# First part of a hybrid-encoder step on one core: TensorE and VectorE taken from the list scheduler and given the order of the source, rewritten as explicit pipelines

## The chip, the core and the metric

The kernel runs on one core of a Trainium2 chip. The metric is the device time of one execution in microseconds (us); the median of 3 runs of the kernel before is 1809.56 us (1807.75 to 1811.77). Below, PE is TensorE, DVE is VectorE, ACT is ScalarE, POOL is GpSimd and SP is SyncE, which issues most of the DMAs.

## The reference

One layer of an encoder is applied to 1024 prompt rows and to 32 rows of a running stream, 1056 rows of 1024 features. All is float32.

```
xn   = rmsnorm(h)
u_a, u_b, v_b, q, k, v, gates = split(xn @ w_in)       # 256,256,256,512,512,512,3*1024
y_a  = GLU(gelu(S5(u_a)))          # 16 groups x 64 complex states, zero-order hold, + d*u
y_b  = u_b * (tril(W_s) @ layernorm(v_b) + b_s)        # chunks of 128 positions, 4 groups
z    = q @ k.T / 8                                     # 8 heads x 64, strictly causal
y_c  = (exp(log_sigmoid(z) + sum of log_sigmoid(-z) over the keys in between)) @ v
h    = h + (sum_i sigmoid(gates_i) * (y_i @ W_i)) @ w_out
h    = h + (silu(rmsnorm(h) @ w_gate) * (.. @ w_up)) @ w_down;   out = rmsnorm(h)
```

The new states, keys, values and normalised v_b rows are outputs too.

## The kernel before, in words

**Numbers.** Every float32 operand of a dense product is split into a rounded high part and the rest (wh and wl for weights, split by ACT at L120 and POOL at L121 out of the buffer raw; xnh and xnl for the normalised rows). A product takes three matmuls (L147, L148, L149). A weight unit is read by SP (L116 or L119), split, and kept in a ring of 4 buffers. "Feature-major" products have up to 512 rows as moving columns (chunks of 512, 272 and 272 rows, 24 matmuls each); "token-major" ones have 256 weight columns (blocks of 128 rows, 24 matmuls each).

**The first part** (the context ph1, up to about 700 us) has these stages:

- norm: per block of 128 rows, DVE scales (L184), PE transposes (L189), ACT copies the high half, DVE subtracts (L194). Then the values: 8 blocks and the sample rows, token-major; ACT writes them to a DRAM buffer v_d.
- keys and queries: four tasks (qk0 to qk3), feature-major; DVE subtracts (qe, L335), SP writes k_d and q_d; keys are transposed back (L310) for the output (kt, L312).
- S5 set-up: some 300 small DVE operations, all issued through the line L455 (the function pump), which end in the tile big; PE transposes big (L629) and craw (L638); later matmuls build KK (L666, L667), and 16 DMAs spread it to D (L684).
- sgu: nine token-major blocks of v_b; DVE normalises each into VN (L412). Beside them runs a chain over the 8 heads: SP loads a head's values and the same values shifted by one row (vda, vdt, L377 and L378), DVE subtracts neighbours (L385, L387), ACT rounds (L388), DVE subtracts (L389), SP writes the head to dv_d (L390). vda and vdt have one buffer each. Then, twice, PE computes u_b (UB) and the mixing pm (L434, L437), for which the PSUM pool "z" has 2 buffers, and DVE forms yt from it (L441, L445).
- ua and s5_main: u_a (ua, L698), the S5 scan and its GLU (yl, za).
- attention: 32 units (pairs of heads x 4 pairs of row blocks x 2), each with scores (PE, ACT sigmoid, DVE scan L862), transposes (L884), the split of the weights (DVE L893) and the product with the head's differences (L901, L902); one sample step near the end (L967 to L1020).

**What fills the gaps.** fill(us) puts steps of the waiting tasks (the keys and queries, then 33 gate products kept for later in DRAM) into the instruction stream; pump puts set-up operations of DVE there.

**What sets the order.** A list scheduler with priorities orders the instructions of all engines after they are written down; it may take a ready instruction ahead of one written earlier. The second part (from L1083 on) is the same in both kernels.

Of the kernel before, what the change touches and what calls it, by code (L numbers as in the profile page):

```python
# [48 lines left out]
def trunk_kernel(ctx: ExitStack, tc: tile.TileContext,  # L49
# [132 lines left out]
    def norm_T(wk, psp, tag, src, dst, gb, rows, hl, off, pair=None):  # L182
        r = rms_rstd(wk, src, rows)
        v.scalar_tensor_tensor(dst, src, r, gb[0:rows], op0=OP.mult, op1=OP.mult)  # L184
        for q in range(2):
            pt = psp.tile([128, 512], F32, name="ptn", tag=tag, bufs=2)
            for e in range(4):
                k = 4 * q + e
                pe.transpose(pt[:, 128 * e:128 * e + rows], dst[:, 128 * k:128 * k + 128], ident[0:rows, 0:rows])  # L189
            pv = pt.rearrange("p (a b) -> p a b", b=128)[:, :, 0:rows]  # L190
            hi = hl[0][:, 4 * q:4 * q + 4, off:off + rows]
            s.activation(hi, pv, AF.Copy)
            lo = hl[1][:, 4 * q:4 * q + 4, off:off + rows]
            v.tensor_sub(lo, pv, hi.bitcast(F32))  # L194
            if pair is not None:
                g.tensor_copy(pair[:, 4 * q:4 * q + 4, 0:32], hi.bitcast(F32))
                g.tensor_copy(pair[:, 4 * q:4 * q + 4, 32:64], lo.bitcast(F32))

    def half_tile(p, name, tag, dt=F32R):
# [7 lines left out]
    with ExitStack() as ph1:  # L207
        ps1 = ph1.enter_context(pool("ps1", 2, PSUM))
        rings.append(ph1.enter_context(pool("ring1", 4)))
        qk = ph1.enter_context(pool("qk", 1))  # L210
        kk = ph1.enter_context(pool("kk", 1))
# [23 lines left out]
        v_units = []  # L235
        with pool("p0", 1) as p0:
            gmix = p0.tile([128, 1024], F32, name="gmix")
            for b in (0, 1, 2, 3, 4, 5, 8, 6, 7):
                t0, rows, h, off = BLOCKS[b]
                xt = p0.tile([128, 1024], F32, name="xt", bufs=3)  # L240
                sp.dma_start(xt[0:rows], x_rows(b))
                if b == 0:
                    sp.dma_start(gmix, dram_bcast(norm_mix, 1024))
                if b < 2:
                    v_units.append(tm_units(win, 1792 + 256 * b))
                xg = p0.tile([128, 1024], F32, name="xg", bufs=2)
                norm_T(p0, ps1, "t", xt[0:rows], xg[0:rows], gmix, rows, xn[h], off, xn2 if b == 8 else None)


        def v_dense(wk):  # L250
            us = v_units
            share = -(-len(pending) // 45)
            z = wk.tile([1, 128], F32, name="vz")
            v.memset(z, 0.0)
            for i in range(4):
                sp.dma_start(v_d[i][0:1, :], z)
            for b, hc in [(b, hc) for b in range(6) for hc in range(2)] + [(b, hc) for hc in range(2) for b in (8, 6, 7)]:
                t0, rows, h, off = BLOCKS[b]
                pump(share)
                if b == 8:  # L260
                    ps = ps_dense()[0:64, 0:256]
                    tm_sample(ps, xn2, us[hc])
                    vs = wk.tile([32, 256], F32, name="v32", bufs=2)
                    add_pair(vs, ps, vs)
                    sp.dma_start(sb_v_s[0, 0, 4 * hc:4 * hc + 4].rearrange("h t d -> t h d"),
                                 vs.rearrange("t (h d) -> t h d", d=64))
                    sp.dma_start(vs_d[:, 256 * hc:256 * hc + 256], vs)
                    continue
                ps = ps_dense()[0:rows, 0:256]
                tm_dense(ps, xn[h], off, rows, us[hc])  # L270
                tc.cur_priority -= SOONER
                v32 = wk.tile([128, 256], F32, name="v32", bufs=2)
                s.activation(v32, ps, AF.Copy)
                s.dma_start(sb_v_p[0, 0, 4 * hc:4 * hc + 4, t0:t0 + 128].rearrange("h t d -> t h d"),
                             v32.rearrange("t (h d) -> t h d", d=64))
                for i in range(2):
                    s.dma_start(v_d[2 * hc + i][1 + t0:129 + t0, :], v32[:, 128 * i:128 * i + 128])
                tc.cur_priority += SOONER
# [17 lines left out]
        def qk_dense(wk, hp):  # L296
# [64 lines left out]
        def sgu(wk, WT, BB, gs):  # L361
# [31 lines left out]
            us = tm_units(win, 512)  # L393
            for b, (t0, rows, h, off) in enumerate(BLOCKS):
# [23 lines left out]
                if b < 8:  # L418
                    load_values(b)
            for ft in range(2):  # L420
                UB = wk.tile([128, T], F32, name="UB", bufs=1)
                unit = fm_unit(win, 256 + 128 * ft)
                for h, o, n, t0 in CHUNKS:
                    ps = ps_dense()[:, 0:n]
                    fm_dense(ps, unit, xn[h], o, n)
                    s.activation(UB[:, t0:t0 + n], ps, AF.Copy)
                for q in range(3):
# [19 lines left out]
                    sp.dma_start(y_d[2 + ft][min(q, 1)][:, o:o + w], yt[:, 0:w])  # L447

# [18 lines left out]
        def s5_setup(pl, keep, out):  # L467
# [7 lines left out]
            v.tensor_copy(rows[32:40, :].rearrange("a (g2 p) -> a g2 p", p=64), lt[32:40, :, None].to_broadcast([8, 2, 64]))  # L475
# [130 lines left out]
            braw = pl.tile([128, 2, 8, 16], F32, name="braw")  # L606
            for n, b in enumerate((ssm_b_re, ssm_b_im)):
                sp.dma_start(braw[:, n], bass.AP(tensor=b.tensor, offset=b.offset, ap=[[16, 128], [2048, 8], [1, 16]]))
# [22 lines left out]
            craw = pl.tile([128, 2, 128], F32, name="craw")  # L631
            for n, c in enumerate((ssm_c_re, ssm_c_im)):
                for g2 in range(2):
                    sp.dma_start(craw[:, n, 64 * g2:64 * g2 + 64],
                                 bass.AP(tensor=c.tensor, offset=c.offset + g2 * 1024, ap=[[2048, 8], [64, 16], [1, 64]]))
# [34 lines left out]
            dr = pl.tile([8, 32], F32, name="dr")  # L670
            sp.dma_start(dr, ssm_d[0].rearrange("(gp c) -> gp c", c=32))
# [15 lines left out]
        def ua_dense(wk):  # L687
            for ft in range(2):
                unit = fm_unit(win, 128 * ft)
# [11 lines left out]
                sp.dma_start(us_d[128 * ft:128 * ft + 128], ua)  # L701

        def s5_main(pl, S):
# [72 lines left out]
            fill(24)  # L776
# [34 lines left out]
        def attention(at, qk_tasks):  # L811
# [28 lines left out]
            def stage_a(hp, tp, h2):  # L840
                kst = heads[hp, h2][0]
                q2 = qs.pop((hp, tp, h2))
                ws = []
                for tt in range(2):
                    i = 2 * tp + tt
                    n = 128 * (i + 1)
                    cs = ((0, max(n, 256)),) if n <= 512 else (((0, 384), (384, 256)) if n == 640 else
                                                             ((0, 384), (384, 384)) if n == 768 else
                                                             ((0, 512), (512, n - 512)))
                    om = at.tile([128, 1024], F32, name="om", bufs=4)  # L850
                    for c0, w in cs:
                        z = ps_tile("z")
                        last = c0 + w >= n
                        pe.matmul(z[:, 0:w], q2[:, 0, 128 * tt:128 * tt + 128], kst[:, c0:c0 + w], start=True, stop=False)
                        pe.matmul(z[:, 0:w], q2[:, 1, 128 * tt:128 * tt + 128], kst[:, c0:c0 + w], start=False, stop=not last)
                        if last:
                            d0 = n - 128 - c0
                            pe.matmul(z[:, d0:d0 + 128], identb, maskb, start=False, stop=True)
                        e = min(w, n - c0)
                        s.activation(om[:, c0:c0 + e], z[:, 0:e], AF.Sigmoid, scale=-0.125)  # L860
                    rev = om[:, 0:n][:, ::-1]
                    v.tensor_tensor_scan(rev, rev, rev, 1.0, op0=OP.mult, op1=OP.bypass)  # L862
                    ws.append(om)
                    yield ws, 2 * n / 2400.0 + 0.06
# [3 lines left out]
            def stage_b(hp, tp, h2, ws):  # L868
                vt = heads[hp, h2][1]
                if h2 == 0:  # L870
# [3 lines left out]
                hl = {}  # L874

                def turn(p):

                    pt = ps_tile("t")
                    diag = p == tp
                    for e in range(4):  # L880
                        if diag and e == 0:
                            continue
                        sb, tt = 2 * p + 1 - e // 2, e % 2
                        pe.transpose(pt[:, 128 * e:128 * e + 128], ws[tt][:, 128 * sb:128 * sb + 128], ident)  # L884
                    lo = 128 if diag else 0
                    if diag:
                        wh, wl = diags[cnt[0] % 2]
                        cnt[0] += 1
                    else:
# [434 lines left out]
```

## Time and profile before

| what | us |
|---|---|
| median of 3 runs | 1809.56 (1807.75 to 1811.77) |
| profiled execution, its own time | 1813.32 |
| its span, first to last instruction | 1811.5 |
| PE busy | 1695.1 (94%) |
| DVE, ACT, POOL busy | 697.2, 516.6, 553.9 |

PE is busy 94% of the span, so a stage is read by the time that PE does not work in it and by what ends that wait. The last stage of the first part ends near 700 us; from there on the two kernels have the same program. "Granted clock" is the share of TensorE's full clock that the chip allowed in a stretch.

### The profile page before, as it was taken

The page shows a single profiled execution, that of the slowest core. Times are in us where ns is not written, and L with a number is a line of the kernel's source. Part 1 is how long each engine was busy: PE and PEld are TensorE (multiplying, and loading weights), DVE is VectorE, ACT ScalarE, POOL GpSimd, SP SyncE. Part 2 cuts the span into 40 slices and gives each one's busy share as a digit, 9 for nine tenths or more (in the row PEclk, how much of TensorE's full clock was granted, in tenths as well). Part 3 has the DMA queues.
Part 4 walks back from the last instruction along what each step waited for, and adds up shares of the span by engine and source line. Part 5 has one row for each costly group of instructions (what it writes and reads, how often), then busy time and mean ns, then how long its engine had stood idle before and what let it go on. Part 6 is the DMA issues. An engine that isn't in the chain of part 4 may idle for free.

```text
span 1811.5 us, 25687 instructions
## 1 busy us (share of the span) xinstructions
PE 1695.1 (94%) x10421; PEld 1503.5 (83%) x10421; DVE 697.2 (38%) x1371; ACT 516.6 (29%) x906; POOL 553.9 (31%) x349
## 2 busy tenths in 40 slices
PE   6989959899899997988999899999999999999997
PEld 6978858677679995788999899889889889888885
DVE  7953621532675651730256601230230220321315
ACT  5322322233555542212323322112112112111124
POOL 2210201243112205435443233233323333333334
PEclk9999979999999998988999999999999999999999
DMA  7454766254655424633362211111111111111102
GB/s 219 119 131 111 186 187 144 94 153 146 192 158 154 124 84 121 222 116 108 105 203 68 73 48 47 47 37 51 41 36 48 46 47 47 47 47 47 47 25 96
DMA packets 242736, 182.12 MB, mean 101 GB/s; under 512 B 59380, under 2 KB 220184, under 8 KB 242616
## 3 DMA queue, kind: packets, MB, share of 16 engines
q1 hardware_dynamic: 214056, 165.25, 31.3%
q10 hardware_dynamic: 28560, 15.21, 2.8%
q8 instruction: 82, 1.34, 0.3%
q14 instruction: 38, 0.31, 0.1%
HBM read 138.66 MB, written 41.18 MB: 99 GB/s over the span
## 4 chain that ended last, share of the span: by engine, by line
PE 49%; DVE 3%; DMA 3%; issue 3%; POOL 2%; ACT 1%; POOLq 0%; SPq 0%; ACTq 0%
PE p L149 16%; PE p L148 16%; PE p L147 16%; POOL wl L121 1%; DMA raw<-y_d 1%; PE p L1266 1%; DVE rs_m L172 1%; DMA raw<-in_w_out_dram 1%; POOL y L1137 1%; DVE rs_m L173 1%; DMA raw<-in_w_branch_c_dram 0%; DMA raw<-in_w_in_dram 0%; PE ptn L189 0%; DVE xb L184 0%; ACT wh L120 0%
## 5 line engine op out<-in xcount | busy, mean ns | idle before, releaser
L121 POOL TENSOR_TENSOR wl<-raw,wh 128x1024 fp32r<-128x1024 f32 x164 | 400.3, 2447 | 871.2 <-ACT wh L120 799.8
L148 PE MATMUL p<-x,wh 128*128 128x272 f32 (+1 forms) x1056 | 342.3, 324 | 0.0
L147 PE MATMUL p<-x,wh 128*128 128x272 f32 (+1 forms) x1056 | 341.5, 323 | 0.0
L149 PE MATMUL p<-x,wl 128*128 128x272 f32 (+1 forms) x1056 | 341.4, 323 | 0.0
L120 ACT ACTIVATE wh<-raw 128x1024 fp32r<-128x1024 f32 x164 | 172.2, 1058 | 445.9 <-PE p L149 182.5
L1222 DVE TENSOR_TENSOR sl<-p,sl 128x272 f32<-128x272 f32 (+1 forms) x66 | 34.6, 525 | 463.8 <-PE p L149 463.8
L147 PEld LDWEIGHTS p<-x,wh 128*128 128x128 f32 x1056 | 198.8, 188 | 16.0
L148 PEld LDWEIGHTS p<-x,wh 128*128 128x128 f32 x1056 | 198.8, 188 | 15.9
L149 PEld LDWEIGHTS p<-x,wl 128*128 128x128 f32 x1056 | 198.5, 188 | 15.3
L147 PE MATMUL p_d<-xnh,wh 128*128 128x272 f32 (+1 forms) x464 | 165.0, 356 | 22.1 <-ACT ua L698 16.0
L149 PE MATMUL p_d<-xnh,wl 128*128 128x272 f32 (+1 forms) x464 | 157.6, 340 | 7.7 <-POOL wl L121 7.7
L148 PE MATMUL p_d<-xnl,wh 128*128 128x272 f32 (+1 forms) x464 | 156.5, 337 | 0.0
L1225 POOL TENSOR_TENSOR act<-sl,act 128x512 fp32r<-128x512 f32 (+2 forms) x66 | 61.0, 924 | 279.6 <-ACT act L1223 279.6
L1276 DVE TENSOR_TENSOR h<-p,h 128x512 f32<-128x512 f32 x160 | 108.2, 687 | 79.3 <-PE p L149 79.3
L148 PE MATMUL p<-wl,act 128*128 128x512 f32 x352 | 137.2, 390 | 1.2 <-POOL wl L121 1.2
L149 PE MATMUL p<-wh,act 128*128 128x512 f32 x352 | 137.1, 389 | 0.0
L147 PE MATMUL p<-wh,act 128*128 128x512 f32 x352 | 136.9, 389 | 0.0
L147 PEld LDWEIGHTS p_d<-xnh,wh 128*128 128x128 f32 x464 | 91.9, 198 | 31.0 <-ACT ua L698 16.4
L862 DVE TENSOR_TENSOR_SCAN om<-om 128x128 f32<-128x128 f32 (+3 forms) x64 | 93.5, 1470 | 30.6 <-ACT om L860 30.4
L149 PEld LDWEIGHTS p_d<-xnh,wl 128*128 128x128 f32 x464 | 91.4, 197 | 16.4 <-POOL wl L121 9.4
L148 PEld LDWEIGHTS p_d<-xnl,wh 128*128 128x128 f32 x464 | 91.6, 197 | 6.7
L1223 ACT ACTIVATE act<-sl 128x272 fp32r<-128x272 f32 (+1 forms) x66 | 32.5, 492 | 191.1 <-DVE sl L1222 191.1
(351 smaller groups left out, 3351.6 us busy)
## 6 DMA issues: line engine op xcount, KB each, us to landing
raw<-in_w_in_dram SPq DMA_DIRECT2D x66, 512.0 KB, 4.0
raw<-in_w_gate_up_dram SPq DMA_DIRECT2D x44, 512.0 KB, 3.8
raw<-in_w_down_dram SPq DMA_DIRECT2D x22, 512.0 KB, 3.5
q<-q_d SPq DMA_DIRECT2D x64, 128.0 KB, 3.1
raw<-in_w_out_dram SPq DMA_DIRECT2D x16, 512.0 KB, 4.5
dv_d<-vdt SPq DMA_DIRECT2D x8, 768.0 KB, 4.3
vt<-dv_d SPq DMA_DIRECT2D x8, 768.0 KB, 6.6
sig_d<-sga ACTq DMA_DIRECT2D x21, 256.0 KB, 2.5
```

Source lines behind the costliest of these rows:

```text
L120: s.activation(wh, raw, AF.Copy)
L121: g.tensor_sub(wl, raw, wh.bitcast(F32))
L147: pe.matmul(ps, ah, bh, start=start, stop=False)
L148: pe.matmul(ps, ah, bl, start=False, stop=False)
L149: pe.matmul(ps, al, bh, start=False, stop=stop)
L172: v.scalar_tensor_tensor(t, y, mh, y, op0=OP.mult, op1=OP.mult)
L173: v.scalar_tensor_tensor(y, t, 1.5, y, op0=OP.add, op1=OP.mult)
L862: v.tensor_tensor_scan(rev, rev, rev, 1.0, op0=OP.mult, op1=OP.bypass)
L1222: v.tensor_mul(sl[:, 0:n], pu, sl[:, 0:n])
L1223: s.activation(act[:, e, t0:t0 + n], sl[:, 0:n], AF.Copy)
L1225: g.tensor_sub(act[:, e, T + TS + t0:T + TS + t0 + p], sl[:, 0:p], act[:, e, t0:t0 + p].bitcast(F32))
L1276: v.tensor_add(hr[:, cs], ps, hr[:, cs])
```

## The change

The first part runs under a manual schedule for PE and DVE: these two engines execute in the order in which the source issues the work. ACT, POOL and SP are still ordered by the list scheduler. The source is rewritten so that this order is a pipeline: the norm of block i+1 is issued ahead of the transposes of block i and the values of block i-1; the S5 set-up's DVE operations start after the norm and stand beside the key and query tasks; the attention issues, per step, a transpose group, the next unit's scores, the held product and a constant amount of gate work. The ring of weight units gets 5 buffers instead of 4, some weights are requested one unit earlier, the small set-up DMAs are issued at its start, and the sample step stands behind the last attention unit.

```diff
     with ExitStack() as ph1:
+        ph1.enter_context(tc.manual_schedule(engines={mybir.EngineType.PE, mybir.EngineType.DVE}))
-        rings.append(ph1.enter_context(pool("ring1", 4)))
+        rings.append(ph1.enter_context(pool("ring1", 5)))
...
+            for i, b in enumerate(order):          # first_norm; takes in v_dense as values(b)
+                if i + 1 < len(order):
+                    scale(order[i + 1])
+                if i + 3 < len(order):
+                    load(order[i + 3])
+                norm_turn(ps1, "t", xgs.pop(b)[0:rows], rows, xn[h], off, xn2 if b == 8 else None)
+                if i:
+                    values(order[i - 1])
...
             def load_values(i):
-                va = wk.tile([128, 12, 64], F32, name="vda")
-                vt = wk.tile([128, 12, 2, 64], F32R, name="vdt")
+                va = vk.tile([128, 12, 64], F32, name="vda")
+                vt = vk.tile([128, 12, 2, 64], F32R, name="vdt")
...
             VN = wk.tile([128, 9, 256], F32, name="VN")
-            us = tm_units(win, 512)
...
+                if b == 7:
+                    unit = fm_unit(win, 256)
...
-            fill(24)                               # s5_main
+            fill(28)
...
-                        fill(1.3)
+                        fill(0.6)
...
+            beside = 2.0                           # attention
+            ws = [scores(units[0], 0), scores(units[0], 1)]
+            fill(2)
+            held = None
             for i, u in enumerate(units):
                 ahead(i + 2)
+                nxt = units[i + 1] if i + 1 < len(units) else None
+                wn = []
+                part = beside / (u[1] + 2)
+                for p in range(u[1] + 1):
+                    now = turn(u, ws, p)
+                    if nxt and len(wn) < 2:
+                        wn.append(scores(nxt, len(wn)))
+                    if held:
+                        apply(*held)
+                    held = now
+                    fill(part)
+                if nxt and len(wn) < 2:
+                    wn.append(scores(nxt, len(wn)))
+                fill(part)
+            fill(2)
+            apply(*held)
+            sample_attention(at, ck)
...
             while tasks and credit[0] > 0:
-                pump(5)
+                pump(3)
...
+                fill(7)
                 next(setup)
                 finish(qk_tasks[1])
+                next(setup)
+                finish(qk_tasks[2])
                 for _ in setup:
                     pass
+                us = tm_units(win, 512)
+                finish(qk_tasks[3])
```

What stands where is best seen in three places of the engines' queues (a row is a line of the source, the operation, output<-inputs and the tile's shape). The first is DVE's queue around the first complex products of the S5 set-up, Pr and Pi. Before, they stand among the last rows of the norm:

```order
L184 SCALAR_TENSOR_TENSOR xg<-xt,rs_m,gmix 128x1024
L194 TENSOR_TENSOR xnl_150<-ptn,xnh_149 128x4x128 x2
L455 TENSOR_TENSOR sm<-sm 128x8 x2
L455 TENSOR_TENSOR Pr<-sm 128x8
L455 TENSOR_TENSOR Pi<-sm 128x8
L455 TENSOR_TENSOR sm<-sm 128x8
L455 TENSOR_TENSOR te<-Pr 128x8
L455 TENSOR_TENSOR te<-Pi 128x8
```

Now the same products stand among the subtractions of the keys and queries (qe, L357), and the set-up's line is L481:

```order
L481 TENSOR_TENSOR Pr<-sm 128x8
L481 TENSOR_TENSOR Pi<-sm 128x8
L481 TENSOR_TENSOR te<-Pr 128x8
L481 TENSOR_TENSOR te<-Pi 128x8
L481 TENSOR_TENSOR Pr<-te 128x8
L481 TENSOR_TENSOR te<-Pr,Pi 128x8
L357 TENSOR_TENSOR qe<-p_av,qe 128x272
```

The set-up's work has moved behind the norm, and its operations stand in the order of the source, each behind the one that it needs.

The second is PE's queue where it transposes big and craw. Before, eight of the sixteen transposes of big stand after the first matmuls of qk1, and matmuls of qk1 between them and the rest:

```order
L147 MATMUL p_av<-xnh_147,wh 128x512
L148 MATMUL p_av<-xnl_148,wh 128x512
L149 MATMUL p_av<-xnh_147,wl 128x512
L629 MATMUL p_z<-ident,big 128x128 x8
L147 MATMUL p_av<-xnh_147,wh 128x512
L629 MATMUL p_z<-ident,big 128x128 x8
L148 MATMUL p_av<-xnl_148,wh 128x512
L638 MATMUL p_z<-ident,craw 128x128 x2
```

Now all of qk0 and qk1 and three matmuls of qk2 stand ahead of them, and the sixteen are in one piece (L663):

```order
L147 MATMUL p_av<-xnh_147,wh 128x512
L148 MATMUL p_av<-xnl_148,wh 128x512
L149 MATMUL p_av<-xnh_147,wl 128x512
L663 MATMUL p_z<-ident,big 128x128 x16
L667 MATMUL p_z<-ident,craw 128x128 x2
L147 MATMUL p_av<-xnh_147,wh 128x512
L148 MATMUL p_av<-xnl_148,wh 128x512
```

About one key and query task more lies ahead of these transposes.

The third is DVE's queue at the first two yt of the sgu stage (numbers behind a name are its buffer's; each head has its own vda). Before, the third head's differences stand ahead of the first yt, and the fourth head's behind the second:

```order
L412 SCALAR_TENSOR_TENSOR VN_1892<-vb_2442,rs_m_2468,gs_488 32x256
L385 TENSOR_TENSOR vda_2077<-vda_2077,vdt_2078 128x512
L387 SCALAR_TENSOR_TENSOR vda_2077<-vdt_2078,last_1890,vda_2077 128x256
L389 TENSOR_TENSOR vdt_2078<-vda_2077,vdt_2078 128x12x64
L441 TENSOR_TENSOR yt_2592<-p_z_2583,BB_487 128x512
L445 TENSOR_TENSOR yt_2592<-yt_2592,UB_2498 128x512
L441 TENSOR_TENSOR yt_2605<-p_z_2596,BB_487 128x512
L445 TENSOR_TENSOR yt_2605<-yt_2605,UB_2498 128x512
L385 TENSOR_TENSOR vda_2153<-vda_2153,vdt_2154 128x512
```

Now the differences ahead of the first yt are the eighth and last head's:

```order
L433 SCALAR_TENSOR_TENSOR VN_2369<-vb_2878,rs_m_2904,gs_1017 32x256
L407 TENSOR_TENSOR vda_2865<-vda_2865,vdt_2866 128x512
L409 SCALAR_TENSOR_TENSOR vda_2865<-vdt_2866,last_2367,vda_2865 128x256
L411 TENSOR_TENSOR vdt_2866<-vda_2865,vdt_2866 128x12x64
L466 TENSOR_TENSOR yt_3024<-p_z_3015,BB_1016 128x512
L470 TENSOR_TENSOR yt_3024<-yt_3024,UB_2930 128x512
L466 TENSOR_TENSOR yt_3037<-p_z_3028,BB_1016 128x512
```

Every yt stands behind all eight heads.

Lines of the new kernel that are named below, with those of the kernel before in brackets: L399 and L400 (L377, L378) loads of a head, L407 to L411 (L385 to L389) its differences, L466 and L470 (L441, L445) yt, L481 (L455) set-up, L663 (L629) transposes of big, L889 (L862) scans, L912 (L893) the split of the attention weights.

## Rows read from the trace of the kernel before

**Rows 1.** Windows: stretch, its length, busy us (instructions) per engine, granted clock, DMA share, GB/s.

```profile
26.00:79.00 53.00, 51.61 (x426) 50.05 (x425) 50.81 (x273) 20.47 (x43) 7.89 (x7) 1.00 0.56 147
79.00:160.00 81.00, 72.82 (x468) 65.72 (x467) 40.45 (x80) 22.20 (x44) 15.61 (x8) 0.96 0.48 121
160.00:304.00 144.00, 119.22 (x771) 108.20 (x770) 58.17 (x163) 40.31 (x94) 21.38 (x9) 0.88 0.64 169
304.00:456.00 152.00, 142.49 (x691) 112.84 (x690) 50.89 (x47) 43.34 (x63) 51.16 (x23) 0.96 0.47 137
456.00:697.00 241.00, 222.85 (x1567) 197.26 (x1566) 153.49 (x170) 119.33 (x239) 41.25 (x31) 0.96 0.45 136
```

**Rows 2.** PE's waits by what ended them, 0 to 456 us: total, times, longest.

```profile
PE p_d L147 <- ACT ua L698: 16.0, 1, 16.0
...
PE p_t L310 <- ACT kt L312: 7.0, 1, 7.0
```

**Rows 3.** PE's waits, 456 to 740 us.

```profile
PE p_t L884 <- DVE om L862: 8.1, 12, 1.9
PE p_t L1006 <- DVE sgs L1004: 5.9, 2, 5.8
```

**Rows 4.** PE's timeline: first key matmul, first sgu matmul (start, duration, instruction).

```profile
78.49 0.40 PE L147 MATMUL p_av<-xnh,wh 128*128 128x512 f32 x1
...
143.69 0.36 PE L147 MATMUL p_d<-wh,xnh 128*128 128x256 f32 x1
```

**Rows 5.** ACT's timeline: two successive value blocks, two successive gate chunks (idle before in brackets).

```profile
57.80 0.38 ACT L273 ACTIVATE v<-p_d 128x256 f32<-128x256 f32 x1 [0.46 <-PE p_d L149]
...
60.66 0.39 ACT L273 ACTIVATE v<-p_av 128x256 f32<-128x256 f32 x1 [2.48 <-PE p_av L149]
...
402.87 0.60 ACT L1032 ACTIVATE sga<-p_d 128x512 f32<-128x512 f32 x1 [4.98 <-PE p_d L149]
...
408.45 0.60 ACT L1032 ACTIVATE sga<-p_d 128x512 f32<-128x512 f32 x1 [4.98 <-PE p_d L149]
```

**Rows 6.** Windows of line L455 alone: stretch, length, DVE busy (instructions), granted clock, DMA.

```profile
60.00:90.00 30.00, 27.81 (x105) 1.00 0.46 124
90.00:110.00 20.00, 10.88 (x18) 0.83 0.46 120
```

**Rows 7.** DVE's timeline in the set-up.

```profile
62.24 0.17 DVE L455 TENSOR_TENSOR sm<-sm 128x8 f32<-128x8 f32 x1
62.44 0.17 DVE L455 TENSOR_SCALAR sm<-sm 128x8 f32<-128x8 f32 x1
...
71.38 2.65 DVE L455 TENSOR_TENSOR te<-Ei 128x256 f32<-128x256 f32 x1
```

**Rows 8.** POOL's timeline at the same time.

```profile
71.35 4.93 POOL L121 TENSOR_TENSOR wl<-raw,wh 128x1024 fp32r<-128x1024 f32 x2 [22.22 <-ACT wh L120]
```

**Rows 9.** Line L385, the eight heads: durations, first and last start.

```profile
L385 DVE TENSOR_TENSOR vda<-vda,vdt x8: 673/692/1294, 173.2 to 262.1; 128x512 f32<-128x512 f32 x8
```

**Rows 10.** DVE's timeline over one period of the head chain.

```profile
251.66 0.69 DVE L385 TENSOR_TENSOR vda<-vda,vdt 128x512 f32<-128x512 f32 x1 [9.72 <-DMA vdt<-v_d]
...
253.66 0.96 DVE L389 TENSOR_TENSOR vdt<-vda,vdt 128x768 fp32r<-128x768 f32 x1 [0.91 <-ACT vdt L388]
262.12 0.69 DVE L385 TENSOR_TENSOR vda<-vda,vdt 128x512 f32<-128x512 f32 x1 [7.50 <-DMA vdt<-v_d]
```

**Rows 11.** SP's queue: spreading KK, the first head's load, and the same period.

```profile
160.56 7.43 SPq L684 DMA_DIRECT2D D<-KK  x9
168.09 0.54 SPq L377 DMA_DIRECT2D vda<-v_d  x1
...
254.65 0.33 SPq L390 DMA_DIRECT2D dv_d<-vdt  x1
...
258.99 0.36 SPq L377 DMA_DIRECT2D vdt<-v_d  x1
```

**Rows 12.** PE in the 5 us after the wait for ua, as in Rows 1.

```profile
265.00:270.00 5.00, 4.83 (x21) 4.83 (x22) 0.20 (x5) 2.04 (x5) 0.00 (x0) 0.50 0.67 265
```

More of the change, by code (lines that the diff above doesn't have):

```diff
@@ L255, in v_dense @@
             for i in range(4):
                 sp.dma_start(v_d[i][0:1, :], z)
-            for b, hc in [(b, hc) for b in range(6) for hc in range(2)] + [(b, hc) for hc in range(2) for b in (8, 6, 7)]:
+            scale(0)
+            for i, b in enumerate(order):
                 t0, rows, h, off = BLOCKS[b]
[L259 to L278, printed above, removed]
@@ L426, in sgu @@
                     s.activation(UB[:, t0:t0 + n], ps, AF.Copy)
+                    if o + n == HALF[0] and not h:
+                        unit_b = fm_unit(win, 0 if ft else 384)
+                unit = unit_b
                 for q in range(3):
@@ L838, in load_q, with scores @@
                 qs[hp, tp, h2] = q2
-            def stage_a(hp, tp, h2):
+            def scores(u, tt):
+                hp, tp, h2 = u
                 kst = heads[hp, h2][0]
[L842 to L864, printed above, removed]
@@ new lines, in scores @@
+                for c0, w in cs:
+                    z = ps_tile("z")
+                    last = c0 + w >= n
+                    pe.matmul(z[:, 0:w], q2[:, 0, 128 * tt:128 * tt + 128], kst[:, c0:c0 + w], start=True, stop=False)
+                    pe.matmul(z[:, 0:w], q2[:, 1, 128 * tt:128 * tt + 128], kst[:, c0:c0 + w], start=False, stop=not last)
+                    if last:
+                        d0 = n - 128 - c0
+                        pe.matmul(z[:, d0:d0 + 128], identb, maskb, start=False, stop=True)
+                    e = min(w, n - c0)
+                    s.activation(om[:, c0:c0 + e], z[:, 0:e], AF.Sigmoid, scale=-0.125)
@@ new lines, in scores, with turn @@
+                rev = om[:, 0:n][:, ::-1]
+                v.tensor_tensor_scan(rev, rev, rev, 1.0, op0=OP.mult, op1=OP.bypass)
+                return om
+            avs = {}
+            def turn(u, ws, p):
+                tp = u[1]
+                pt = ps_tile("t")
+                diag = p == tp
+                for e in range(4):
+                    if diag and e == 0:
+                        continue
+                    sb, tt = 2 * p + 1 - e // 2, e % 2
+                    pe.transpose(pt[:, 128 * e:128 * e + 128], ws[tt][:, 128 * sb:128 * sb + 128], ident)
+                lo = 128 if diag else 0
+                if diag:
+                    wh, wl = diags[cnt[0] % 2]
+                    cnt[0] += 1
+                else:
+                    wh = at.tile([128, 512], F32R, name="wth", bufs=2)
+                    wl = at.tile([128, 512], F32R, name="wtl", bufs=2)
+                s.activation(wh[:, lo:512], pt[:, lo:512], AF.Copy)
+                v.tensor_sub(wl[:, lo:512], pt[:, lo:512], wh[:, lo:512].bitcast(F32))
+                return u, p, wh, wl
@@ L1050, in finish @@
                 fill(1.0)
-        qk_tasks = [qk_dense(qk, hp) for hp in range(4)]
-        tasks.extend(qk_tasks)
-        tasks.extend(gate_ahead(qk, h, m) for h in range(2) for m in range(AHEAD[h]))
+        with pool("p0", 1) as p0:
+            rest = first_norm(p0)
+            rest()
         with pool("s5k", 1) as s5k:
             sgc = sgu_consts(s5k)
-            with pool("s5t", 1) as s5t, pool("pv", 1) as pv:
+            with pool("s5t", 1) as s5t, pool("kk", 1) as kk:
+                qk_tasks = [qk_dense(qk, kk, hp) for hp in range(4)]
+                tasks.extend(qk_tasks)
+                tasks.extend(gate_ahead(qk, h, m) for h in range(2) for m in range(AHEAD[h]))
                 S = {}
```

209 lines of the change are left out of this document (95 added, 114 removed).

## The prediction, written before the new kernel ran

> **What bounds the kernel now.** I read the page first: PE is busy 94% of 1811.5 us, so the time is PE's work plus the time in which it waits or runs at a low clock. The second part is the same in both kernels, so only the first 700 us count. The windows by stage come next [rows 1]: the reader is to take PE's busy time from each length. Behind the start PE lacks 1.4, 8.2, 24.8 and 9.5 us up to 456 us, together 44 us, and 18 us more in the attention up to 697 us. The list of PE's waits says what ended them: the largest is one wait of 16.0 us for ACT's copies of ua, the next of one piece 7.0 us for kt [rows 2]; in the attention they are 8.1 us for scans and 5.9 us for the sample step [rows 3].
>
> What stands behind the 16.0 us is seen in the head chain. DVE's differences of the last head start at 262.12 us, having waited 7.50 us for the DMA of vdt [rows 10]; ACT rounds them and then copies ua, in order, and PE goes on at 265 us. The chain of eight heads takes from 173.2 to 262.1 us [rows 9], a mean period of 88.9/7 = 12.7 us. One undisturbed period is 262.12 - 251.66 = 10.46 us [rows 10]: 3.0 us until the head is written (SP's issue at 254.65), 4.3 us until vdt may be loaded again (258.99), 3.1 us for the load [rows 11]. It is a serial loop through one buffer, and the change keeps the one buffer.
>
> **The change part by part.** PE does the same products before and after; some 22 matmuls of gates move from behind 456 us to ahead of it (22 x 5.58/24 = 5 us by the gate chunks' pitch [rows 5]), which cancels. So I compare waits, stage by stage.
>
> *Start and norm.* In the new order VectorE does only norm here, PE the transposes of one block and the values of the one before. PE was busy 51.6 of 53 us [rows 1]; there is nothing to gain but 1.4 us. I take the same end, 78.5 us, when the first key matmul starts [rows 4].
>
> *Set-up (wait A).* Before, the set-up's 300 or so DVE operations lay beside the norm and the values and used DVE's holes. Now they start behind the first 7 us of key matmuls, at 78.5 + 7.8 = 86.3 us, and PE transposes big after qk0 and qk1. A task is 2 x (5.58 + 2 x 2.97) us (the 272-row chunk by its share of the 512-row one [rows 5]) and 1.4 us of transposes, 24.5 us; PE is there at 78.5 + 2 x 24.5 + 0.7 = 128.2 us.
> DVE's queue up to the last big holds 235 set-up operations: 198 of at most 64 columns, 12 of 128, 6 of 256, 18 of 512 and one of 1072. The 198 follow one another at 0.20 us where one needs the one before [rows 7], at about 0.1 us where not; source order has mostly pairs, so I take 0.165 us, 33 us. The larger ones, by the 0.69 us of 512 columns [rows 9] scaled with the columns, are 20 us. Nine qe and four small copies in between are 5.5 us. Where POOL splits weights, DVE operations of 0.3 to 0.4 us took up to 2.65 us [rows 7, 8]; POOL splits a unit for each half task, so three to five such delays of 2.2 us fall in this stretch, 7 to 11 us. Together 86.3 + 33 + 20 + 5.5 + 7 = 152 us at the least of the delays: wait A is 152 - 128 = 23 us. Bounds: at 0.09 us per small operation 137 us, 9 us of wait; at 0.20 us and five delays 163 us, 35 us. Line L455 was busy 27.8 of 30 us where DVE had little else [rows 6], so a mean near the dependent spacing is the nearer one; I keep 23. The cover that is gone is the norm stage.
>
> *sgu (wait B).* Call S the moment PE starts sgu (143.69 us before [rows 4]). The first head's load used to wait on SP behind the spreading of KK, 7.43 us for nine DMAs [rows 11]; in the new SP queue the tail of that spreading still stands ahead of it, ten DMAs of 0.83 us, and two weight reads. Its load takes 173.2 - 168.1 = 5.1 us [rows 9, 11]. The first differences are then at about S + 16 (S + 6 if the ten are through before S). Seven periods follow. With p = 11.2 us, between the clean 10.46 and the mean 12.7, the eighth head ends at S + 16 + 78.4 + 3 = S + 97.
> Before, this length cost 16 us only, since after the third head DVE took the first yt and PE went on with UB, pm and ua. Now DVE's queue has all eight heads ahead of the first yt. The pool "z" holds two pm, so PE may compute two and then has nothing that it may do out of order. Until there it has nine token-major blocks (8 x 2.9 + 1.9 = 25 us by [rows 5]), some 63 matmuls of fill (15 us), UB (5.58 + 2 x 2.97 = 11.5 us) and two pm (2 us): it is through at S + 54 or so. Wait B is 97 - 54 = 43 us; I take 40, since PE's blocks are themselves held a little by DVE's queue. Bounds: start at S + 6 and p = 10.46 give 28 us, p = 12.7 with S + 16 gives 54 us. What is queued behind the waiting subtraction on DVE is yt, and behind yt on PE the rest of UB, ua and the whole S5.
>
> Here the Trainium skill, "DMA: Bandwidth & Descriptors", section "Anatomy of one DMA", speaks for a shorter period: it fits one DMA as 2.0 us and its bytes at 436 GB/s (measured on the GpSimd path). The 786 KB of a head would then take an estimated 3.8 us, against 4.3 us in the trace, and the load of 390 KB 2.9 us against 3.1. By that estimate p is 9.7 us, B is 30 us and the sum below about 10 us lower.
>
> *S5.* PE lacked 9.5 us between 304 and 456 us [rows 1]. In source order the rest of the final states, the large subtraction yl and the reading of U stand in PE's or DVE's way in turn; the fills are 28 instead of 24 and 0.6 instead of 1.3. I take 12 us (bounds 5 and 18).
>
> *Clock.* At granted clocks of 0.96, 0.88 and 0.96 over PE's busy 72.8, 119.2 and 142.5 us [rows 1], low clock costs 2.9 + 14.3 + 5.7 = 22.9 us before. After the 16 us wait, the granted clock was 0.50 for 5 us [rows 12], a loss of 2.5 us. The new kernel has two long waits (5 us), and I keep 2.9 and 5.7 for the short ones: 13.6, a gain of 9 us.
>
> *Attention and sample.* DVE is busy 153 of 241 us [rows 1], so it follows PE. The waits were 14 us [rows 3]; the constant fill gives long units (four pairs of blocks) no more gate work than short ones. I take 0 with bounds of -8 (scan waits gone) and +8.
>
> *Sum,* against the profiled execution's 1813.3 us: gone are the 44 us of waits; new are A 23, B 40 and S5 12; the clock gives 9. 23 + 40 + 12 - 44 - 9 = +22, 1835 us. The median of the runs stands 3.8 us under the profiled execution, so I predict **1832 us**. With the bounds, the low case (A 9, B 28, S5 9, attention -8) is 9 + 28 + 9 - 44 - 9 - 8 = -15, 1795 us; the high one (A 30, B 50, S5 16) is 1852 us.
>
> **The rivals.**
> *Faster.* The head chain could run short, if its DMAs meet less traffic once the keys and queries are written: with loads at S + 6 and p = 8 us, B is 6 + 56 + 3 - 54 = 11 us, and with A at 15 the sum is 15 + 11 + 12 - 44 - 9 = -15: about 1795 us, and 1785 if the scan waits go too. The sign turns where A + B falls under 41 us. For it speaks that three of the long periods before had ua's and the queries' DMAs beside them; against it, that in the undisturbed period DVE's own part was already only 3.0 of 10.46 us [rows 10, 11]. Chance 0.25.
> *No change.* A + B of 41, within 3.6 us (0.2%, about what a measurement of this kernel can tell): 1806 to 1813 us. Chance 0.07.
> *Slower still.* The attention becomes VectorE's: a long unit has two scans of up to 1024 columns, four splits and a sum, and 2.0 us of gates beside it instead of a share of its cost. If eight long units lose 1.5 us each, 12 us come on top: about 1845 us. For it speaks DVE's share of 64% there [rows 1], against it that the scans ended only 8.1 us of waits [rows 3]. Chance 0.12.
> *That the order isn't what it says* is no rival: both queues are fixed by the source, as their rows show.
>
> **How the numbers follow.** The forecast has 0.56. Slower is the forecast and the third rival, 0.68; faster 0.25; the same 0.07. The range 1790 to 1855 reaches from just under the faster rival's middle to the high case; for the forecast alone it is 1815 to 1852 us.
>
> **What would show it.** In the new profile PE must have one wait near 128 us that DVE's big ends (15 to 30 us), and one behind the second pm that DVE's yt ends (27 to 54 us), with DVE's L407 waiting for vdt eight times, 10.5 to 12.7 us apart; the 16.0 us wait for ua and the 7.0 us for kt must be gone. The sum of PE's waits between 79 and 480 us would be near 75 us. I am wrong if DVE finishes big before 140 us, if the first head is loaded while the keys still run, or if PE has other work in its queue between UB and the third pm.

## The result and the profile after

The new kernel takes 1881.19 us (median of 4, 1878.10 to 1886.61) against 1808.65 us: a ratio of 1.0404 (95% interval 1.0372 to 1.0436), 72.5 us slower. Slower was forecast, with 1832 us. The profiled execution took 1879.09 us, 65.8 us more than that of before.

The windows by stage, first before, then after, with the borders at sgu's first matmul, at the reading of U, at the first scores and at the end of the sample step:

```profile
79.00:143.30 64.30, 57.30 (x360) 51.47 (x358) 38.98 (x75) 19.96 (x41) 14.98 (x7) 0.95 0.53 138
143.30:320.60 177.30, 151.35 (x950) 135.61 (x949) 60.37 (x171) 45.39 (x101) 22.01 (x10) 0.90 0.61 157
320.60:456.00 135.40, 125.89 (x620) 99.68 (x620) 50.16 (x44) 40.51 (x59) 51.16 (x23) 0.95 0.44 135
```

```profile
79.00:206.90 127.90, 107.02 (x659) 94.96 (x658) 81.89 (x291) 34.47 (x71) 24.39 (x12) 0.93 0.53 131
206.90:372.40 165.50, 108.26 (x681) 95.86 (x680) 53.52 (x153) 37.87 (x77) 27.20 (x12) 0.86 0.56 142
372.40:522.00 149.60, 135.38 (x604) 108.69 (x604) 51.09 (x44) 35.67 (x54) 43.50 (x19) 0.83 0.35 109
522.00:758.00 236.00, 212.89 (x1546) 191.07 (x1545) 154.83 (x171) 115.56 (x236) 34.40 (x28) 0.97 0.45 131
```

Length less PE's busy time is PE's wait: set-up and keys 7.0 before and 20.9 after, sgu and ua 26.0 and 57.2, S5 9.5 and 14.2, attention and sample 18.2 [rows 1] and 23.1 us. The second row of each also shows what changed in sgu: 950 matmuls and 151 us of work lay there before, now 681 and 108 us. PE's waits up to 456 us, to be read beside [rows 2]:

```profile
PE p_d L147 <- DVE vb L139: 32.0, 1, 32.0
PE p_z L663 <- DVE big L481: 13.3, 3, 9.5
...
PE p_av L147 <- ACT vb L427: 8.1, 1, 8.1
PE p_z L742 <- DMA U<-us_d: 7.5, 1, 7.5
...
PE p_z L773 <- DVE fin L771: 4.8, 1, 4.8
PE p_d L135 <- ACT vb L427: 4.5, 1, 4.5
```

The wait for ua is gone. In its place are three waits on the v_b blocks (vb), 44.6 us together. The longest ends when VectorE's sum of the last v_b block (L139) frees a PSUM buffer; that sum stands behind the differences of the seventh head, which had waited for their load:

```profile
299.76 0.69 DVE L407 TENSOR_TENSOR vda<-vda,vdt 128x512 f32<-128x512 f32 x1 [4.20 <-DMA vdt<-v_d]
302.75 0.41 DVE L139 TENSOR_TENSOR vb<-p_d,jk 32x256 f32<-32x256 f32 x1
```

```profile
303.31 0.57 PE L147 MATMUL p_d<-xnh,wh 128*128 128x272 f32 x1 [31.95 <-DVE vb L139]
```

The head chain as in [rows 9], and SP's queue ahead of it as in [rows 11]:

```profile
L407 DVE TENSOR_TENSOR vda<-vda,vdt x8: 683/693/1924, 231.3 to 311.7; 128x512 f32<-128x512 f32 x8
```

```profile
209.57 6.44 SPq L711 DMA_DIRECT2D D<-KK  x10
216.10 2.06 SPq L116 DMA_DIRECT2D raw<-in_w_in_dram  x2
218.43 0.72 SPq L399 DMA_DIRECT2D vda<-v_d  x1
219.20 1.66 SPq L400 DMA_DIRECT2D vda<-v_d  x1
220.91 1.12 SPq L399 DMA_DIRECT2D vdt<-v_d  x1
```

The first head starts 24.4 us behind sgu's first matmul (206.9), the period is 80.4/7 = 11.5 us. The first head did not wait for its load: VectorE's view of L407 has seven waits for vdt for eight heads. It stood behind the normalisation of two v_b blocks, and the first of these was late, since ACT copied it only behind a gate's sigmoid (sga) whose product PE finished near 221 us; here are ACT, then VectorE:

```profile
221.01 0.60 ACT L1040 ACTIVATE sga<-p_av 128x512 f32<-128x512 f32 x1 [11.44 <-PE p_av L149]
222.05 0.39 ACT L427 ACTIVATE vb<-p_d 128x256 f32<-128x256 f32 x1 [0.43 <-ACT sga L1040]
```

```profile
222.56 0.15 DVE L428 TENSOR_SCALAR st<-st 128x1 f32<-128x1 f32 x1 [13.81 <-ACT vb L427]
```

Last, the S5 output products (99 and 98 matmuls from the final states' transpose on), before and after:

```profile
353.70:371.80 18.10, 18.10 (x99) 13.82 (x97) 0.28 (x1) 5.47 (x8) 5.42 (x3) 0.95 0.22 62
```

```profile
410.20:441.10 30.90, 30.90 (x98) 23.18 (x98) 0.32 (x2) 2.42 (x5) 0.00 (x0) 0.50 0.05 16
```

The same work takes 12.8 us more at a granted clock of 0.50, the lower of TensorE's two levels (1.2 and 2.4 GHz).

### The profile page after: what moved, and what is told of

Read it like the earlier page. It is cut to its first block, busy times and chain, and to the rows that moved or that the text cites. A ratio compares the mean times of both kernels' runs of the same rounds, so it can differ in the third digit from the quotient of the medians.

```text
span 1877.4 us, 25690 instructions
## 1 busy us (share of the span) xinstructions
PE 1699.2 (91%) x10421; PEld 1510.6 (80%) x10421; DVE 708.2 (38%) x1370; ACT 516.5 (28%) x906; POOL 557.3 (30%) x350
## 4 chain that ended last, share of the span: by engine, by line
PE 66%; DVE 13%; DMA 8%; issue 5%; ACT 4%; POOL 2%; SPq 1%; ACTq 0%; POOLq 0%; DVEq 0%
PE p L149 16%; PE p L148 16%; PE p L147 15%; PE p_d L147 2%; PE p_d L148 2%; PE p_d L149 2%; DVE om L889 2%; DMA dv_d<-vdt 2%; POOL wl L121 2%; DVE sm L481 1%; DMA vdt<-v_d 1%; PE p_av L147 1%; PE p_t L903 1%; DMA raw<-y_d 1%; PE p_av L148 1%
## 5 line engine op out<-in xcount | busy, mean ns | idle before, releaser
L147 PE MATMUL p_d<-xnh,wh 128*128 128x272 f32 (+1 forms) x440 | 147.6, 335 | 35.6 <-DVE vb L139 32.0
L148 PE MATMUL p_d<-xnl,wh 128*128 128x272 f32 (+1 forms) x440 | 145.0, 329 | 0.0
L149 PE MATMUL p_d<-xnh,wl 128*128 128x272 f32 (+1 forms) x440 | 144.5, 328 | 0.0
L147 PEld LDWEIGHTS p_d<-xnh,wh 128*128 128x128 f32 x440 | 84.8, 193 | 42.8 <-issue 32.7
L889 DVE TENSOR_TENSOR_SCAN om<-om 128x128 f32<-128x128 f32 (+3 forms) x64 | 95.6, 1496 | 21.7 <-ACT om L887 21.4
L149 PEld LDWEIGHTS p_d<-xnh,wl 128*128 128x128 f32 x440 | 84.6, 192 | 6.8
L148 PEld LDWEIGHTS p_d<-xnl,wh 128*128 128x128 f32 x440 | 84.9, 193 | 5.5
```

Source lines behind the costliest of these rows:

```text
L147: pe.matmul(ps, ah, bh, start=start, stop=False)
L148: pe.matmul(ps, ah, bl, start=False, stop=False)
L149: pe.matmul(ps, al, bh, start=False, stop=stop)
```

## The experiments

The four runs of the new kernel lie between 1878.10 and 1886.61 us, so a single run beside it is read to about 4 us either way.

**Which engine's order.** Three runs of the new source: `engines={PE}`, `engines={DVE}`, and no manual schedule.

> The new source with only TensorE in source order; VectorE is ordered by the list scheduler again. Theory (VectorE's order): the scheduler takes the v_b blocks and the yt ahead of waiting head differences and the set-up beside the queries, so that sgu loses 20 us of wait instead of 50 and the set-up 13 us less: about 1835 us. Rival (TensorE's order): what costs is that TensorE may not go past a product that waits; then it stays at 1870 us or more.

> The new source with only VectorE in source order; TensorE is ordered by the list scheduler. Theory (VectorE's order): the chain of heads still stands ahead of the yt, so the waits in sgu stay near 40 us, with a little gate work moved into them: 1860 to 1880 us. Rival (TensorE's order): the scheduler finds other products for TensorE in these waits: 1830 us or less.

> The new source without the manual schedule on either engine. Both theories: most of the loss is the fixed order, not the rewritten source: 1800 to 1830 us. Rival (source): the set-up behind the norm, the constant gate work in the attention and the sample step at the end cost by themselves: 1840 us or more.

Measured: 1851.88, 1871.28 and 1836.44 us. TensorE alone in order lies between its theory and its rival, VectorE alone in its theory's range. VectorE's order costs 29 us beside TensorE's, TensorE's alone 15, both 45. But 1836 us is still 28 us above the kernel before: the expectation of both theories was too low, and over a third of the loss is in the rewritten source. Where it lies is seen in the windows of the run without a manual schedule: set-up and keys, sgu and ua, and the S5 output products.

```profile
79.00:197.00 118.00, 104.69 (x649) 93.69 (x649) 77.05 (x284) 33.85 (x71) 24.52 (x11) 0.93 0.55 137
197.00:350.90 153.90, 129.66 (x789) 113.47 (x787) 56.29 (x153) 40.88 (x83) 29.77 (x13) 0.92 0.65 166
384.60:415.50 30.90, 30.86 (x98) 23.17 (x98) 0.28 (x1) 4.42 (x7) 4.68 (x2) 0.50 0.12 35
```

PE waits 13.3 us in the set-up (7.0 before), but 24.2 us in sgu and ua, no more than before (26.0). The output products are at half clock here too, and the second part starts with a wait of 14.7 us (5.8 before). So the source brings these costs and half of the set-up's; the additional wait in sgu comes from the order. Neither engine's order brings it alone: between sgu's first matmul and the reading of U, PE waits 24.2 us with neither engine in source order, 34.3 with VectorE, 37.4 with TensorE and 57.2 with both. Where the list scheduler orders TensorE, 789 matmuls lie in that stretch, else 681.

In the two runs with VectorE under the list scheduler the blocks pass and the wait is for ua again, as it was before (16.0 us); the first line is TensorE alone in order, the second the list scheduler on both. With VectorE alone in order, the third line, PE waits for the blocks:

```profile
PE p_d L147 <- ACT ua L726: 28.3, 1, 28.3
```

```profile
PE p_av L147 <- ACT ua L725: 21.6, 1, 21.6
```

```profile
PE p_z L459 <- DVE VN L433: 12.6, 4, 8.3
```

So VectorE's order decides where the chain of heads is waited for, and TensorE's order takes away the work that would lie beside it.

**Two buffers, one buffer of weights less, and the ring alone.**

```diff
-        rings.append(ph1.enter_context(pool("ring1", 5)))
+        rings.append(ph1.enter_context(pool("ring1", 4)))
-            with pool("sgu", 1) as sg, pool("vd", 1) as vk:
+            with pool("sgu", 1) as sg, pool("vd", 2) as vk:
```

> The new kernel with two buffers each for vda and vdt (the ring of weights goes back to 4 buffers to make room). Theory (head chain): PE's 50 us of waits between the start of sgu and the second pm come from the eight heads that go through one buffer ahead of the first yt and of the v_b blocks in VectorE's source order. With two buffers a head's load runs beside the head before it, the period falls from 11.5 us to 4 to 7 us, and the waits of sgu fall to 10 to 20 us: about 1845 us against 1879. Rival (ring): PE waits for weights and its own order; the period may fall but the waits stay above 40 us, and one ring buffer less makes it 1880 us or more.

> The new kernel with 4 buffers in the ring of weights instead of 5, for comparison with the runs that needed the room. If the fifth buffer matters, 5 to 10 us slower than the new kernel; otherwise the same, 1878 to 1886 us.

Measured: 1864.05 us with both edits, 1881.47 us with the ring alone, which therefore costs nothing. The period falls to 6.9 us:

```profile
L407 DVE TENSOR_TENSOR vda<-vda,vdt x8: 673/685/687, 230.2 to 278.5; 128x512 f32<-128x512 f32 x8
```

```profile
PE p_av L147 <- ACT wh L120: 32.8, 1, 32.8
```

The gain, 17 us against the ring of 4, is half of what was expected, and PE's waits from sgu to U are 44.6 us, as the rival had it (above 40), though not its time of 1880 us. The weights that PE now waits for are read by SP behind the last heads (274.63 us) and split by ACT behind the last L410 (280.34 us). So in SP's and ACT's queues, too, what stands behind the heads waits for them.

**Heads spread out, heads early.** The first moves five of eight heads behind UB, and the two memsets of ua from VectorE to GpSimd; the second, with the ring of 4, starts the chain right behind big. Its edit, in part (head_on() finishes the head that is loaded, if one is, and loads the next):

```diff
                 next(setup)
+                head_on()
+                fill(11)
+                head_on()
+                fill(11)
+                head_on()
                 finish(qk_tasks[2])
...
+                fill(8)
+                head_on()
+                fill(11)
+                head_on()
                 finish(qk_tasks[3])
```

> The new kernel, both engines in source order, with the heads spread out: three beside the v_b blocks, one behind the first UB, four behind the second; the two memsets of ua go to GpSimd so that VectorE's queue holds nothing of ua behind the last heads. One buffer as before. Theory (head chain in VectorE's queue): the waits of sgu fall from 50 to about 15 us, and some 10 us come back where S5's first VectorE work stands behind the last heads: about 1855 us. Rival (SP and weights): the weights that TensorE waits for stand behind the heads' DMAs on SP in any order, so that the waits stay above 35 us: 1870 us or more.

> The new kernel, both engines in source order, one buffer for the heads, but the chain of heads starts beside the third and fourth key and query task, right behind big (the values are ready since 79 us); four heads are through before sgu, the others stand between its blocks. The ring of weights has 4 buffers for want of room. Theory (cover): the new source has finished all keys and queries before sgu, so that only some 58 us of TensorE work lie beside a chain of 107 us; with the chain moved to where TensorE has 55 us more, the waits from sgu to the reading of U fall from 57 to about 20 us: about 1840 us. Rival (queue): a waiting head holds up the key and query subtractions behind it on VectorE wherever it stands; the waits turn up there, 1865 us or more.

Measured: 1875.40 and 1864.76 us. Later, the wait in the blocks falls to 13.4 us, but 28.9 us come back at ua, and PE's waits from sgu to U are still 52 us: moving the heads behind gains 6 us at most, little beyond the spread. Early, the waits from sgu to U fall from 57 to 35 us and the time by 17 us against the ring of 4. That is half of what was expected, and the time is the rival's (1865 us): part of the wait turns up on the queries (QS, 7.8 us). Both runs fit a chain that needs TensorE work beside it, whatever its place among VectorE's work.

**The set-up.** One key and query task more ahead of big, and one ahead of KK.

```diff
-                finish(qk_tasks[1])
+                finish(qk_tasks[2])
                 next(setup)
-                finish(qk_tasks[2])
+                us = tm_units(win, 512)
+                finish(qk_tasks[3])
                 for _ in setup:
                     pass
-                us = tm_units(win, 512)
-                finish(qk_tasks[3])
```

> The new kernel with one more key and query task ahead of the transposes of big, and one ahead of KK. Theory (set-up): the waits of 13 us at these transposes go, since VectorE is through with big near 150 us and PE then comes at about 153 us; KK comes just ahead of sgu. About 1866 us. Rival: VectorE's queue is the bound of the whole stretch, so that the wait turns up again at KK or in sgu, where the first head's load stands on SP behind the spreading of KK: 1876 to 1885 us.

Measured: 1886.64 us; the rival holds. The 13 us at big go, but sgu starts at 204.3 instead of 206.9 us, only 2.6 us earlier, since PE now waits for qe behind the set-up's operations. These are lost again behind it: from sgu to U it takes 174.6 instead of 165.5 us.

**The final states.**

```diff
             cmul(v, Q[:, 0], Q[:, 1], Z[:, 0], Z[:, 1], Er, Ei, X[:, 0], X[:, 1])
-            fill(12)
+            fill(19)
```

> The new kernel with 7 us more gate work ahead of the transpose of the final states (fill(12) to fill(19)). Theory (clock): the wait of 4.8 us in front of that transpose lets the granted clock fall to 0.50, and the S5 output products behind it, which have no gate work among them, stay at it: 98 matmuls take 31 us instead of 18. With the wait covered both go: 4.8 + 13 = 18 us, about 1861 us. Rival: those products are slow by their own order, and only the wait goes: about 1874 us.

> The same with 7 us more gate work ahead of the transpose of the final states. If the two costs are separate, this takes off what the earlier run of that edit took off, 9 us: about 10 us below the run with the early heads alone. If the clock is low there for another reason, the S5 output products stay at 31 us and nothing is gained.

Measured: 1869.92 us, 9 to 11 us less than the new kernel, and 1844.91 us, 20 us less than with early heads alone, where 10 were expected. The stage did what was expected:

```profile
416.60:433.90 17.30, 17.30 (x99) 13.22 (x98) 0.32 (x2) 2.43 (x6) 1.92 (x1) 1.00 0.16 47
```

So with the wait covered both the wait and the half clock go; the rival, that the products are slow by their own order, is out for the new source. The first run gains less than the 18 us of its stage: PE waits 3.4 us more for yh and 2.1 more for U. With no gates left, the sample step's second group waits 5.4 us more, but the wait ahead of the second part is 5.2 us shorter (9.4).

**The sample step** ahead of the last two units.

> The new kernel with the sample step ahead of the last two attention units instead of behind them. Theory (end of the first part): the 14.6 us wait of PE ahead of the second part's first branch product comes from the sample step's place, whose outputs are read back behind it; it falls to the 6 us of the kernel before: about 1870 us. Rival: it comes from the buffers that the second part takes over, and stays: about 1879 us.

Measured: 1883.22 us. The wait at the start of the second part falls from 14.6 to 10.2 us, 2.8 us come back at the next transposes, and nothing is gained in all. The trace of the new kernel shows the path of that wait: SP reads the weights of the branches at 786.4 us, behind eight reads of y_d that start at 760.5 us, right behind the sample step's writes (758.1). Why these reads take longer than before is open.

**The kernel before, with early heads,** and then with the final states later: by larger fills, and by priority.

```diff
+                    v_dense(pv)
+                    head_on()
+                    finish(qk_tasks[0])
+                    next(setup)
+                    head_on()
+                    fill(12)
+                    head_on()
+                    finish(qk_tasks[1])
+                    head_on()
...
+                if b in (1, 4, 7):
+                    head_on()
...
+            tc.cur_priority += 340
             pt = ps_tile("z")
             pe.transpose(pt[0:32, 0:128], fin.rearrange("p a b -> p (a b)"), ident)
```

> The kernel before (list scheduler on all engines) with its chain of heads started right behind the values instead of in sgu (craw takes tb's room). Theory (chain): its 16.0 us wait for ua has the same cause, the last heads in ACT's and VectorE's queues, and goes; with the clock behind it that is 10 to 18 us: 1791 to 1799 us. Rival: the heads' DMAs then collide with the keys' and queries' and with the small set-up operations, and the time stays at 1809 us or goes above it.

> The kernel before with its heads early, as in the run ahead of this, and 10 us more gate work ahead of the transpose of the final states (fill(12) to fill(22)). Theory (clock): in the run ahead of this the 16 us that the heads gave came back as a wait of 8 us there and as 12.8 us of the S5 output products at half clock; both go: 1784 to 1792 us. Rival: gate work spent here is missing in the attention and at the sample step, which then wait as long: 1800 to 1805 us.

> The same, with the gate work taken from the two fills behind (24 to 20 and 1.3 to 0.9) so that the attention keeps its share. If the supply of gate work decides, this is up to 5 us faster than the run without; if the waits for yh and yl grow in its place, it is the same or slower.

> The kernel before with early heads; the transpose of the final states and the S5 output products get a priority 340 lower, so that the list scheduler puts about 50 gate matmuls (11.6 us) ahead of them, which a larger fill in the source did not do. Theory (clock): the wait of 8 to 10 us and the half clock behind it both go, the output products take 18 instead of 31 us, and 5 us of it may come back where gate work is missing later: 1785 to 1793 us. Rival: the half clock comes from these small products themselves, or the gates are missing later for as long: 1798 to 1805 us.

> The same with 400 instead of 340, about 75 gate matmuls (17 us) ahead. Theory: the wait is covered with more room, and the time is within 4 us of the run with 340, since work is only moved. Rival (supply): each gate matmul moved here is missing later, 6 us more than in the run with 340.

| run | median us | ratio to before, 95% interval |
|---|---|---|
| early heads | 1804.45 | 0.9976 (0.9966 to 0.9987) |
| and fill 22 | 1805.24 | 0.9980 (0.9967 to 0.9993) |
| and less behind | 1804.91 | 0.9983 (0.9971 to 0.9995) |
| early heads, priority 340 | 1804.10 | 0.9945 (0.9920 to 0.9970) |
| early heads, priority 400 | 1813.38 | 1.0013 (0.9995 to 1.0031) |

The theories had expected gains of 10 to 25 us; by the medians beside the kernel before, four runs gain 3.5 to 6 us (0.2 to 0.35%), and the one with 400 loses 3. (The ratio for 340 also weighs in three executions of the kernel before of 1822 to 1826 us; that of the medians is 0.9966.) The 16 us wait for ua goes (the chain runs from 93.7 to 216.4 us), but most of it is given back in S5: with early heads alone, an 8.0 us wait ahead of the final states and the output products at half clock.

```profile
PE p_z L754 <- DVE Q L761: 8.0, 1, 8.0
```

```profile
328.60:359.30 30.70, 30.70 (x97) 23.08 (x97) 0.28 (x1) 4.27 (x7) 4.68 (x2) 0.50 0.12 35
```

The larger fills left the same 150 matmuls between the reading of U and that transpose (151, 151 and 150 in the three runs): the list scheduler did not follow them. The priority of 340 moved 50 matmuls there (201) and the wait went, but not the half clock. It also put gate matmuls among the products, so that their sequence is not the same; these are the products' first 9 us and the rest:

```profile
335.00:344.00 9.00, 8.83 (x44) 6.12 (x42) 0.05 (x1) 3.08 (x5) 2.79 (x2) 1.00 0.29 90
344.00:372.00 28.00, 27.57 (x75) 18.00 (x75) 0.00 (x0) 4.29 (x7) 6.61 (x3) 0.54 0.22 66
```

The clock fell near 346 us, in the midst of them; the waits in front were 0.6 us at 344 and 1.5 us at 331. My theory that a wait ahead decides is so far not enough: covering it kept the clock up in both runs of the new source and not here. With 400, an 8.4 us wait for a PSUM copy came between the products.

## Why the prediction was wrong

The direction and the places were right, the size was not: +22 us was the sum, +65.8 us is measured.

- *sgu (wait B)* is the step that failed most. It put 40 us in place of 26, +14; measured is 57.2 for 26.0, +31. The period was right (11.2 forecast, 11.5 measured). The start was S + 24 and not S + 16, and the eighth head ended at S + 109 and not S + 97. Two queues set that start, almost together. On SP the ten DMAs to D end at 216.0, the two weight reads at 218.2, and the last piece of the first head is issued only at 225.4 us. In the later heads VectorE went on 2.7 to 4.2 us behind that issue, so the first load was there near 228 to 230 us (an estimate). VectorE came to it at 231.3 us, held by the v_b block that ACT had copied late. PE's own work up to the third pm was 60 us and not 54, which leaves 50 us of wait there. The other 7.5 us are ua's way through DRAM to U, which was not in the sum: before, a query task and gates lay over it.
  The place of PE's stop was wrong as well, though it cost little: not behind two pm, but already behind the first of UB's three chunks, for the PSUM buffer shown above. The rest of UB and the two pm then ran beside the eighth head, and the wait for yt itself was only 3.0 us.
- *Clock* was forecast as 9 us gained, and the S5 output products at half clock were in no term: this is the second step that failed. They cost 12.8 us. PE's busy time as a whole is 4.1 us longer (1699.2 for 1695.1), so the rest of it came out 8.7 us shorter; where, no run shows. The reckoning was loose, too: I had multiplied the mean granted clock of a window with its busy time, but that mean holds the waits, in which a low clock costs nothing. From 272 to 304 us PE was busy for 0.69 us, at a mean of 0.54:

```profile
272.00:304.00 32.00, 0.69 (x3) 0.72 (x4) 13.58 (x46) 5.29 (x14) 0.00 (x0) 0.54 0.60 150
```

  In slices of 0.5 us the same working gives 18.7 us of loss for the kernel before where the prediction had 22.9 (an estimate from its trace, 79 to 456 us), so this made 4 us.
- *Set-up (wait A)* held: 23 us forecast, 20.9 measured, as 13.3 at big and the rest at kt, QS and qe. VectorE was through with big at 153.0 us (forecast 152); PE came to it at 136.7 us and not 128, for it had waited at the others first. In the working, the larger operations add up to 18 us and not 20, which changes nothing.
- *S5* held in its waits (12 against 14.2 us).
- *Attention and the end* were put at 0. Measured are 5 us more in the attention and sample, and about 6 us more in all behind it, where the first branch product waits 14.6 instead of 5.8 us; the start of the second part was in no term.
- *The range* was too narrow by its own bounds: its high case took A 30, B 50 and S5 16, not the 35, 54 and 18 given for them, and left out the +8 for the attention. With these it ends near 1871 us, still below the measured time.

The misses add up, from sgu, clock, set-up, S5, attention and end: 17 + 13 - 2 + 2 + 5 + 6 and 2 us of the norm are 43 of the 44 us. That the set-up and S5 came out near their forecasts is the sum of several waits each, not one wait of the forecast size. The rival "faster" needed loads at S + 6 and a head period of 8 us; with two buffers the period was 6.9 us, the loads were as late as before (first head at 230.2 us), and the waits from sgu to U stayed at 44.6 us.

## What to carry to other kernels

A serial chain through one buffer was hidden here only by work that needed none of its results, in every queue that it passed: count that work, not the chain's place. Where an engine is set to source order, list what stands behind each of its waiting instructions, down to the PSUM buffers that it drains, for there the next engine stops. A fill in the source is an order only where the engine follows the source; under the list scheduler two larger fills changed nothing. And run a rewritten source once without its new order: what remains of the loss is the source's own.

## What was not expected of the hardware

The S5 output products (98 small matmuls, PE busy throughout) ran in 17 to 18 us at a granted clock of 0.95 to 1.00 in three kernels (the one before, and the two with more gate work ahead of the final states), and in about 31 us at 0.50 or 0.51 in thirteen, with the same instructions. In the thirteen, PE had waited 4.6 to 10.2 us right ahead of them, and the clock came back only with the large gate matmuls behind them. In the kernel before, where PE had waited 2.5 us and the clock was at 0.50 for 3.5 us, it rose in their midst, near 355.5 us. With priority 340 it fell in their midst, with gate matmuls among them and no such wait in front. What decides stays open.
